# The second MLP product as seven block products

## The chip, the cores and the metric

The kernel runs on one core of one Trainium2 chip. The metric is the device time of one execution in microseconds (us). Lower is better.

## The reference

One layer of a hybrid decoder on a sequence of 512 tokens and a model width of 1,024, all in float32. Three token mixers (pooling, a gated convolution, dilated attention) feed a gated sum and the product with `w_o`. The change concerns what follows it:

```
x = x + merged @ w_o
h2 = rms_norm(x, norm_mlp)
x = x + jnp.square(jax.nn.relu(h2 @ w_ff1)) @ w_ff2      # w_ff1 1024 x 4096, w_ff2 4096 x 1024
```

## The kernel before, in words

Everything lies transposed, channels on the 128 partitions and the 512 tokens along the free dimension. Each float32 matmul is done as three in the `fp32r` type: a tile is split into a high part (a copy on ScalarE that rounds, `hi`) and a low part (a subtraction on VectorE, `lo`), and the product is high by high, high by low, low by high. `split` (L127) does this for a weight unit of 128 x 1024, into tiles `wh` and `wl` with three buffers each; `mm3` (L134) issues the three matmuls. Weight units come over SP's queue into `raw` tiles, three buffers.

The residual is `res`, eight tiles of 128 x 512. After the product with `w_o`, whose last four chunks (`wo_chunk`, 24 matmuls of 512 columns each) end one after the other, `x2_evac` (L682) adds a chunk to the residual on VectorE and writes a copy scaled by the norm's gain, `hs`, on ScalarE. `rs2.add` squares the residual on ScalarE and sums on VectorE.

The first MLP product (L781 to L840) is done by seven block products instead of eight, in eight groups of 512 hidden channels. The forms of the activations (P1, P2, Q3 to Q7, each a block or a sum of blocks of `hs`, split into high and low) are made once. For each group the forms of the weights are made as they go: B11, B12, B21 and B22 are the four 512 KB blocks of a group. One sum of two blocks is made on VectorE (`u`), three others by a DMA on POOL's queue that accumulates into the tile (`wx`, three buffers, or `wy`, two). `order()` gives the order of the products, `w_fill` makes forms `FORMS_AHEAD` (2) ahead of use, and `product` issues 24 matmuls of 256 columns: for eight 128 x 128 weight blocks the three of high and low. Evacuations follow Q6, Q7, P2 and Q4; they apply the relu, the norm and the square and leave the hidden activations `f` in SBUF. VectorE and ScalarE run in written order from the first `x2_evac` to Q4 of group 0; after that a planner orders them by its own costs.

The second MLP product (L820 to L862) is a plain one. For each of 32 tiles of `f` it loads a unit of `w_ff2`, splits both, and issues 8 x 3 matmuls of 512 columns into eight PSUM banks, one bank for each 128 output channels. Five banks of the first tile are begun between Q7 and Q4 of the last group (`EARLY`). The last three tiles are done bank by bank (`TAIL`), so that a bank can be added to the residual and stored while the next one is finished.

Of the kernel before, what the change touches and what calls it, by code (L numbers as in the profile page):

```python
# [18 lines left out]
P = 128  # L19
D = 1024  # L20
S = 512
# [45 lines left out]
def hybrid_layer(ctx: ExitStack, tc: tile.TileContext, xT, wst, pmix, vecs, consts, outT):  # L67
# [59 lines left out]
    def split(raw, pool):  # L127
        hi = pool.tile([P, 1024], F32R, tag="wh", name=nm("wh"))
        lo = pool.tile([P, 1024], F32R, tag="wl", name=nm("wl"))
# [401 lines left out]
    for m in range(KC):  # L531
        gt = []
        for n in range(3):
# [7 lines left out]
            pump()  # L541
        if m == 0:
# [4 lines left out]
            lp = right(front, "lp")  # L547
            for k in range(KC):
                t = rp.tile([P, S], F32, name=f"res{k}")
                nc.scalar.dma_start(t, xT[:, k, :])  # L550
                res.append(t)
# [38 lines left out]
    fpool = right(back, "fpool", reuse_waits="tile")  # L590
    sm = ExitStack()
# [20 lines left out]

    NG = NFF // 4

    def order():
# [7 lines left out]
        yield from [("Q6", NG - 1), ("Q4", NG - 2), ("Q7", NG - 1), ("Q4", NG - 1)]  # L623
# [7 lines left out]
    def w1_forms():  # L631
# [8 lines left out]
        for kind, g in order():  # L640
# [22 lines left out]
            elif kind == "Q4":  # L663
                yield xt[g]

    forms = w1_forms()
    ready = deque()

    def w_fill(n):
        while len(ready) < n:  # L670
# [3 lines left out]
            ready.append(split(t, wpool))  # L674

    def w_form():
        w_fill(FORMS_AHEAD + 1)
# [13 lines left out]
    def split_form(kind, t, ks, sign=1.0):  # L691
        if kind not in sx:
            sx[kind] = [spool.tile([P, 4, H], F32R, name=f"{kind}{part}") for part in "hl"]
# [37 lines left out]
    def late(kind, g):  # L731
# [7 lines left out]
        elif (kind, g) == ("Q5", 0):  # L739
            split_form("Q6", s2, HIGH)  # L740
            for m in range(5, KC):
# [37 lines left out]
    outs, fs, ws = [], [], []  # L779
    EARLY = 5  # L780
    for kind, g in order():  # L781
# [25 lines left out]
        elif kind == "Q6":  # L807
            q.R = bank()
            product(kind, q.R, True, True)
            q.v = tmp()  # L810
            nc.vector.tensor_tensor(q.v, q.R, q.x1, OP.subtract)
            nc.vector.tensor_tensor(q.f[:, 2:4, :H], halves(q.v), halves(q.T), OP.add)
        elif kind == "Q7":
# [6 lines left out]
            if g == NG - 1:  # L820
                n_loaded[0] = base + NFF
                end[0] = wst.shape[0]
                ws.append(unit())
                both = fpool.tile([P, 1024], F32R, tag="wx", bufs=3, name=nm("f0"))
# [131 lines left out]
```

## Time and profile before

| | |
|---|---|
| median of 3 runs | 819.49 us (819.14 to 821.77) |
| profiled execution | 818.48 us, of which the span from the first to the last instruction is 816.7 us |
| mean granted TensorE clock | 0.994 of full speed |
| TensorE / VectorE / ScalarE busy | 98% / 60% / 41% of the span |
| DMA | 93.66 MB, 115 GB/s over the span |

The span is what the views of the trace show, and the time of the execution is 1.8 us longer. PE is TensorE, PEld its weight loads, DVE VectorE, ACT ScalarE, POOL GpSimd and SP SyncE; a letter q behind an engine is its queue. An arrow `<-` stands between what an instruction writes and what it reads. In brackets behind an instruction stands how long its engine was idle before it, and which instruction released it.

### The profile page before, as it was taken

What the parts mean: (1) busy time and instruction counts of PE and PEld (TensorE: products, weight loads), DVE (VectorE), ACT (ScalarE), POOL (GpSimd) and SP (SyncE); (2) the same over time, 40 slices, a digit from 0 to 9 for tenths busy, and PEclk for the clock granted to TensorE, in tenths of its full rate; (3) what the DMA queues carried; (4) which work ended last, traced back from release to release, by engine and by line L of the source; (5) the groups of instructions that cost most, each with busy time, mean ns of one, the idle gap of its engine ahead of it and who ended that gap; (6) DMA issues with size and microseconds to landing.
All of it is one profiled execution on the core that took longest, in us unless ns stands there. A gap on an engine that the chain in (4) does not pass through costs nothing.

```text
span 816.7 us, 10396 instructions
## 1 busy us (share of the span) xinstructions
PE 801.2 (98%) x4225; PEld 679.9 (83%) x4225; DVE 488.3 (60%) x608; ACT 336.2 (41%) x432; POOL 71.9 (9%) x67
## 2 busy tenths in 40 slices
PE   8999998999999999999999989999999999999998
PEld 5787787887888888888888878999999888888886
DVE  7758686776895434543445588887777633233323
ACT  6375255742363222222222665555564433223320
POOL 4320012124200000000000011111110000000000
PEclk9999999999999999999999989999999999999999
DMA  7323221222244222333232266877775322332312
GB/s 253 129 79 104 77 78 52 91 84 72 78 147 164 77 85 101 101 103 102 78 103 78 104 170 139 234 183 187 187 181 115 130 86 95 104 98 83 103 52 103
DMA packets 28271, 93.66 MB, mean 115 GB/s; under 512 B 3264, under 2 KB 3520, under 8 KB 28224
## 3 DMA queue, kind: packets, MB, share of 16 engines
q1 hardware_dynamic: 23472, 78.19, 28.2%
q0 software_dynamic: 3456, 12.58, 9.3%
q10 hardware_dynamic: 1296, 2.23, 0.9%
q8 instruction: 33, 0.54, 0.3%
q14 instruction: 14, 0.11, 0.0%
HBM read 90.90 MB, written 2.10 MB: 114 GB/s over the span
## 4 chain that ended last, share of the span: by engine, by line
PE 89%; DVE 5%; ACT 3%; issue 2%; DMA 1%; SPq 0%; DVEq 0%; ACTq 0%
PE bank L137 23%; PE bank L138 23%; PE bank L139 23%; PE bank L761 5%; PE bank L760 5%; PE bank L762 5%; ACT wh L130 1%; DVE wl L131 1%; DMA mg<-xT 1%; DVE wl L233 1%; PE bank L393 1%; PE bank L357 1%; DVE xs L178 1%; ACT hs L684 0%; PE bank L392 0%
## 5 line engine op out<-in xcount | busy, mean ns | idle before, releaser
L130 ACT ACTIVATE wh<-raw 128x1024 fp32r<-128x1024 f32 x120 | 126.9, 1057 | 297.3 <-PE bank L138 156.1
L131 DVE TENSOR_TENSOR wl<-raw,wh 128x1024 fp32r<-128x1024 f32 x120 | 148.4, 1237 | 131.7 <-ACT wh L130 131.4
L137 PE MATMUL bank<-xs,wh 128*128 128x512 f32 x464 | 183.0, 395 | 1.1 <-ACT tmp L206 1.1
L139 PE MATMUL bank<-xs,wl 128*128 128x512 f32 x464 | 181.9, 392 | 1.3 <-DVE wl L233 1.2
L138 PE MATMUL bank<-xs,wh 128*128 128x512 f32 x464 | 182.2, 393 | 0.6 <-DVE xs L179 0.6
L137 PEld LDWEIGHTS bank<-xs,wh 128*128 128x128 f32 x464 | 87.1, 188 | 22.3 <-ACT tmp L206 1.6
L139 PEld LDWEIGHTS bank<-xs,wl 128*128 128x128 f32 x464 | 87.2, 188 | 21.4 <-DVE wl L233 2.5
L138 PEld LDWEIGHTS bank<-xs,wh 128*128 128x128 f32 x464 | 87.2, 188 | 19.9 <-DVE xs L179 1.3
L139 PE MATMUL bank<-tmp,wl 128*128 128x512 f32 x248 | 97.6, 394 | 0.0
L138 PE MATMUL bank<-tmp,wh 128*128 128x512 f32 x248 | 97.2, 392 | 0.0
L137 PE MATMUL bank<-tmp,wh 128*128 128x512 f32 x248 | 95.6, 389 | 0.0
L537 DVE TENSOR_TENSOR tmp<-bank,rstd 128x512 f32<-128x512 f32 x24 | 16.6, 692 | 66.8 <-PE bank L139 66.8
L138 PEld LDWEIGHTS bank<-tmp,wh 128*128 128x128 f32 x248 | 46.5, 188 | 11.0 <-DVE tmp L419 0.2
L137 PEld LDWEIGHTS bank<-tmp,wh 128*128 128x128 f32 x248 | 46.6, 188 | 10.3
L139 PEld LDWEIGHTS bank<-tmp,wl 128*128 128x128 f32 x248 | 46.5, 188 | 9.6 <-DVE wl L131 0.3
L130 ACT ACTIVATE wh<-wx 128x1024 fp32r<-128x1024 f32 x24 | 25.4, 1059 | 24.1 <-PE bank L761 22.4
L563 DVE TENSOR_TENSOR tmp<-tmp,bank 128x512 f32<-128x512 f32 x24 | 16.5, 688 | 26.5 <-PE bank L139 26.5
L138 PE MATMUL bank<-br,wh 128*128 128x512 f32 x80 | 31.4, 393 | 0.0
L137 PE MATMUL bank<-br,wh 128*128 128x512 f32 x80 | 31.3, 391 | 0.0
L648 POOL DMA_DIRECT2D wx<-wst x8 | 7.2, 900 | 273.2 <-DVE P2l L697 255.1
L139 PE MATMUL bank<-br,wl 128*128 128x512 f32 x80 | 31.1, 389 | 0.0
L131 DVE TENSOR_TENSOR wl<-wx,wh 128x1024 fp32r<-128x1024 f32 x24 | 29.3, 1222 | 2.2 <-ACT wh L130 1.7
(217 smaller groups left out, 1468.4 us busy)
## 6 DMA issues: line engine op xcount, KB each, us to landing
raw<-wst SPq DMA_DIRECT2D x128, 512.0 KB, 3.3
wx<-wst POOLq DMA_DIRECT2D x16, 512.0 KB, 5.7
wy<-wst SPq DMA_DIRECT2D x8, 512.0 KB, 5.1
wy<-wst POOLq DMA_DIRECT2D x8, 512.0 KB, 5.4
raw<-wst SPq DMA_DIRECT2D x8, 256.0 KB, 5.4
mg<-xT SPq DMA_DIRECT2D x8, 256.0 KB, 5.5
res<-xT ACTq DMA_DIRECT2D x8, 256.0 KB, 4.2
outT<-res SPq DMA_DIRECT2D x7, 256.0 KB, 2.0
```

The costliest lines, as they stand in the source:

```text
L130: nc.scalar.activation(hi, raw, AF.Copy)
L131: nc.vector.tensor_tensor(lo, raw, hi.bitcast(F32), OP.subtract)
L137: nc.tensor.matmul(out, wh[:, cols], xh, start=start, stop=False)
L138: nc.tensor.matmul(out, wh[:, cols], xl, start=False, stop=False)
L139: nc.tensor.matmul(out, wl[:, cols], xh, start=False, stop=stop)
L178: nc.vector.tensor_scalar(hi, raw, gain, None, op0=OP.mult)
L233: tc.keep_in_program_order(nc.vector.tensor_tensor(lo[:, half], raw_w[kk][:, half], hi[:, half].bitcast(F32), OP.subtract))
L537: nc.vector.tensor_tensor(t, b, rstd, OP.mult)
L563: nc.vector.tensor_tensor(t, t, b, OP.mult)
L760: nc.tensor.matmul(o, wh[:, w], xh[:, k], start=first, stop=False, skip_group_check=True)
L761: nc.tensor.matmul(o, wh[:, w], xl[:, k], start=False, stop=False, skip_group_check=True)
L762: nc.tensor.matmul(o, wl[:, w], xh[:, k], start=False, stop=last, skip_group_check=True)
```

## The change

The second MLP product is done by seven block products a group too. A group takes 512 hidden channels of `f` (four tiles of 128), its blocks are 256 channels by 256 tokens on the side of the activations, and 256 hidden by 512 output channels of `w_ff2` on the other. The activation forms are now made for each group: `a_sum` makes the differences on VectorE (q5, q6, q3, q7), `a_split` the high and low parts, five buffers each. The weight forms are made as in the first product, by the same generator, in a stream that goes on from one product into the other; `order()` is longer by 56 products, p1, q5, q6 and q4 of all groups first, then p2, q3 and q7. The four accumulators (A, T, R, X) fill two PSUM banks each and stay there over all groups. B22 of the second product is loaded into five buffers, two `wy` and three `wx`. Every fourth weight form of the new product goes into the tiles that the activation form Q7 had, so there are four buffers for them and three forms ahead.

From Q6 of the last group on, VectorE, ScalarE and TensorE run in written order. p1(0) lies between Q4 of group 6 and Q7 of group 7, and q5(0) between Q7 and Q4 of group 7. After the last group of p1 and q5, ScalarE copies A and T (`keep`). The evacuation of an accumulator adds it to quarters of the residual and stores them. q7 of the last two groups is done output chunk by output chunk.

At the first product's start, the scaled copies `hs` are made on VectorE by `tensor_scalar`, four chunks are evacuated before P1 is split and the fifth after it, sums of squares of the first four follow, and the table load of ScalarE goes from L710 to right behind the last sigmoid.

```diff
-    def split(raw, pool):
+    def split(raw, pool, tags=("wh", "wl"), **kw):
...
+        if m == KC - 1:
+            tc.keep_in_program_order(nc.scalar.preload_act_table_set("natural_log_exp_and_others"))
...
+            res_all = rp.tile([P, KC, S], F32, name="res")
...
-        yield from [("Q6", NG - 1), ("Q4", NG - 2), ("Q7", NG - 1), ("Q4", NG - 1)]
+        n = NG - 1
+        yield from [("Q6", n), ("Q4", n - 1), ("p1", 0), ("Q7", n), ("q5", 0), ("Q4", n)]
+        yield from [("p1", 1), ("q5", 1), ("q6", 0)]
+        for g in range(2, NG):
+            yield from [("p1", g), ("q5", g), ("q6", g - 1), ("q4", g - 2)]
+        yield from [("p2", 0), ("q6", n), ("q4", n - 1), ("q3", 0), ("p2", 1), ("q4", n), ("q3", 1), ("q7", 0)]
+        for g in range(2, NG):
+            yield from [("p2", g), ("q3", g), ("q7", g - 1)]
+        yield ("q7", n)
...
+            elif kind == "p1":
+                bt[g] = raw_unit()
+                nc.sync.dma_start(bt[g], w2_block(g, B11))
+                yield bt[g]
+            elif kind == "q5":
+                b12 = raw_unit()
+                nc.sync.dma_start(b12, w2_block(g, B12))
+                xt[g] = wx()
+                nc.vector.tensor_tensor(xt[g], bt[g], b12, OP.add)
+                yield xt[g]
+                nc.gpsimd.dma_start(xt[g], w2_block(g, B22), accum_op=OP.add)
+            elif kind == "q6":
+                yield xt[g]
+                nc.gpsimd.dma_start(xt[g], w2_block(g, B21), accum_op=OP.add)
+            elif kind == "q4":
+                yield xt[g]
+            elif kind == "p2":
+                z = raw_unit()
+                nc.sync.dma_start(z, w2_block(g, B21))
+                yield z
+            elif kind == "q3":
+                yt[g] = wy() if g in (0, 1, 5, 6) else wx()
+                nc.sync.dma_start(yt[g], w2_block(g, B22))
+                yield yt[g]
+                nc.gpsimd.dma_start(yt[g], w2_block(g, B12), accum_op=OP.add)
+            elif kind == "q7":
+                yield yt[g]
...
     def w_fill(n):
-        while len(ready) < n:
+        while len(ready) < n and (len(ready) < 3 or n_form[0] >= more):
...
-            ready.append(split(t, wpool))
+            k = n_form[0] - more
+            if k >= 0 and k % 4 == 0:
+                ready.append(split(t, late_forms, ("Q7h", "Q7l"), bufs=1))
+            else:
+                ready.append(split(t, wpool))
+            n_form[0] += 1
 
     def w_form():
-        w_fill(FORMS_AHEAD + 1)
+        w_fill(FORMS_AHEAD + (1 if opool is None else 2))
...
     def x2_evac(m):
         nc.vector.tensor_tensor(res[m], res[m], wo_banks[m], OP.add)
-        nc.scalar.activation(hs[m // 4][:, m % 4], res[m], AF.Copy, scale=vec[:, V_NF + m:V_NF + m + 1])
+        nc.vector.tensor_scalar(hs[m // 4][:, m % 4], res[m], vec[:, V_NF + m:V_NF + m + 1], None, op0=OP.mult)
...
-    tc.keep_in_program_order(nc.scalar.preload_act_table_set("natural_log_exp_and_others"))
...
-    for m in range(5):
+    for m in range(4):
         x2_evac(m)
     split_form("P1", a11, ALL)
+    x2_evac(4)
+    for m in range(4):
+        rs2.add(res[m], nc.vector)
     x2_evac(5)
-    for m in range(5):
-        rs2.add(res[m], nc.vector)
...
+    def a_split(kind, g):
+        hi, lo = (opool.tile([P, 2, H], F32R, tag=tag, bufs=5, name=nm(tag)) for tag in ("ah", "al"))
+        nc.scalar.activation(hi, sums[kind, g], AF.Copy)
+        nc.vector.tensor_tensor(lo, sums[kind, g], hi.bitcast(F32), OP.subtract)
+        return hi, lo
...
+    def a_fill(n):
+        while len(a_ready) < n and n_split[0] < len(second):
+            while n_sum[0] < min(n_split[0] + 2, len(second)):
+                a_sum(*second[n_sum[0]])
+                n_sum[0] += 1
+            a_ready.append(a_split(*second[n_split[0]]))
+            n_split[0] += 1
...
+        if w is None:
+            a_fill(FORMS_AHEAD + 2)
+            w, x = w_form(), a_ready.popleft()
+        (wh, wl), (xh, xl) = w, x
+        for c in chunks if chunks != range(4) else [None]:
+            for kk in range(2):
+                for cc in range(4) if c is None else [c]:
+                    o = banks[i][cc // 2][:, cc % 2 * H:(cc % 2 + 1) * H]
+                    wc = cols(4 * kk + cc)
+                    first, last = opens and kk == 0 and cc % 2 == 0, g == NG - 1 and kk == 1
+                    nc.tensor.matmul(o, wh[:, wc], xh[:, kk], start=first, stop=False, skip_group_check=True)
+                    nc.tensor.matmul(o, wh[:, wc], xl[:, kk], start=False, stop=False, skip_group_check=True)
+                    nc.tensor.matmul(o, wl[:, wc], xh[:, kk], start=False, stop=last, skip_group_check=True)
...
         elif kind == "Q6":
+            if g == NG - 1:
+                ordered = ExitStack()
+                ordered.enter_context(tc.manual_schedule(engines={
+                    mybir.EngineType.DVE, mybir.EngineType.Activation, mybir.EngineType.PE}))
             q.R = bank()
             product(kind, q.R, True, True)
+            if g == NG - 1:
+                sm.close()
+                opool = right(back, "opool", reuse_waits="tile")
+                a_fill(1)
...
         elif kind == "Q4":
             product(kind, q.R, False, True)
+            if g == NG - 2:
+                a_fill(FORMS_AHEAD)
...
+        elif kind == "q7" and g >= NG - 2:
+            a_fill(FORMS_AHEAD + 2)
+            held.append((w_form(), a_ready.popleft()))
+            if g == NG - 1:
+                for b in range(2):
+                    res_add(1, 1, b, snap["x1", b], OP.subtract)
+                    res_add(1, 0, b, snap["x1", b])
+                    res_add(1, 1, b, snap["x5", b])
+                    res_add(1, 0, b, pair(banks["X"][b]))
+                for b in range(2):
+                    for c in (2 * b, 2 * b + 1):
+                        for gg, (w, x) in zip((NG - 2, NG - 1), held):
+                            product2(kind, gg, [c], w, x)
+                    res_add(1, 1, b, pair(banks["R"][b]))
+                    store(1, 1, b, nc.sync)
+                    res_add(1, 0, b, pair(banks["R"][b]), OP.subtract)
+                    store(1, 0, b, nc.scalar)
...
+                    elif kind == "p2":
+                        res_add(0, 0, b, pair(banks["A"][b]))
+                        store(0, 0, b, nc.sync)
+                    elif kind == "q3":
+                        res_add(0, 1, b, pair(banks["T"][b]))
+                        store(0, 1, b, nc.sync)
...
-        if k < NFF - TAIL:
-            for m in range(EARLY if k == 0 else 0, KC):
-                mm3(outs[m], ws[k], cols(m), fs[k], k == 0, False)
-    for m in range(KC):
-        for k in range(NFF - TAIL, NFF):
-            mm3(outs[m], ws[k], cols(m), fs[k], False, k == NFF - 1)
-        parts = [slice(0, S)] if m < KC - 1 else [slice(0, S // 2), slice(S // 2, S)]
-        for t, eng in zip(parts, (nc.sync, nc.scalar)):
-            nc.vector.tensor_tensor(res[m][:, t], res[m][:, t], outs[m][:, t], OP.add)
-            eng.dma_start(outT[:, m, t], res[m][:, t])
```

Names in lower case (p1, q5 and so on) are the products of the second MLP product, those in upper case of the first; the number behind, as in q5(0), is the group. Where the text speaks of the first half of the new product it means p1, q5, q6 and q4 of all groups, and p2, q3 and q7 are the second half.

## Rows read from the trace of the kernel before

**Rows 1.** The page's first part: busy time, share of the span, instructions.
```profile
PE 801.2 (98%) x4225; PEld 679.9 (83%) x4225; DVE 488.3 (60%) x608; ACT 336.2 (41%) x432; POOL 71.9 (9%) x67
```

**Rows 2.** The page's fourth part: the chain that ended last, by engine.
```profile
PE 89%; DVE 5%; ACT 3%; issue 2%; DMA 1%; SPq 0%; DVEq 0%; ACTq 0%
```

**Rows 3.** Windows: length, busy PE, PEld, DVE, ACT, POOL, clock, DMA share, GB/s.
```profile
460.00:480.00 20.00, 17.40 (x92) 15.34 (x91) 15.45 (x20) 11.43 (x18) 0.51 (x1) 0.83 0.21 70
...
540.00:560.00 20.00, 20.00 (x172) 20.00 (x171) 15.30 (x17) 10.37 (x11) 2.59 (x3) 1.00 0.79 191
...
680.00:700.00 20.00, 20.00 (x89) 16.38 (x89) 7.20 (x8) 6.33 (x8) 0.00 (x0) 1.00 0.25 83
```

**Rows 4.** Timeline of TensorE: start, length, instruction, wait before it.
```profile
465.66 0.39 PE L137 MATMUL bank<-mg,wh 128*128 128x512 f32 x1
...
467.03 0.28 PE L760 MATMUL bank<-P1h,wh 128*128 128x256 f32 x1
...
469.74 0.28 PE L762 MATMUL bank<-P1h,wl 128*128 128x256 f32 x1
471.92 0.49 PE L760 MATMUL bank<-P1h,wh 128*128 128x256 f32 x1 [1.91 <-ACT wh L130]
...
488.80 1.12 PE L214 MATMUL bank<-tmp,ones 128*128 128x512 f32 x2
...
508.59 0.39 PE L760 MATMUL bank<-P1h,wh 128*128 128x256 f32 x1 [0.87 <-ACT wh L130]
```

**Rows 5.** Windows of 2 us at two waits of TensorE, columns as above.
```profile
474.00:476.00 2.00, 2.00 (x11) 2.00 (x11) 0.80 (x2) 1.24 (x3) 0.00 (x0) 0.50 0.64 262
508.00:510.00 2.00, 0.96 (x5) 0.74 (x6) 1.43 (x2) 1.49 (x2) 0.00 (x0) 1.00 0.00 0
```

**Rows 6.** Timeline of VectorE.
```profile
457.11 1.23 DVE L697 TENSOR_TENSOR P1l<-hs,P1h 128x1024 fp32r<-128x1024 f32 x1 [4.21 <-ACT P1h L695]
...
488.80 1.23 DVE L131 TENSOR_TENSOR wl<-wx,wh 128x1024 fp32r<-128x1024 f32 x1
...
509.71 1.22 DVE L638 TENSOR_TENSOR wx<-raw,raw 128x1024 f32<-128x1024 f32 x1
510.85 1.22 DVE L131 TENSOR_TENSOR wl<-wx,wh 128x1024 fp32r<-128x1024 f32 x1
511.99 0.68 DVE L834 TENSOR_TENSOR f<-tmp,bank 128x512 f32<-128x512 f32 x1
512.58 1.22 DVE L131 TENSOR_TENSOR wl<-wx,wh 128x1024 fp32r<-128x1024 f32 x1
...
520.99 0.69 DVE L771 SCALAR_TENSOR_TENSOR f<-bank,rstd 128x512 f32<-128x512 f32 x1 [0.31 <-PE bank L762]
...
608.62 0.69 DVE L834 TENSOR_TENSOR f<-tmp,bank 128x512 f32<-128x512 f32 x1 [0.16 <-PE bank L762]
609.34 0.69 DVE L771 SCALAR_TENSOR_TENSOR f<-f,rstd 128x512 f32<-128x512 f32 x1
...
631.23 0.69 DVE L834 TENSOR_TENSOR f<-tmp,bank 128x512 f32<-128x512 f32 x1 [0.28 <-PE bank L762]
...
812.95 0.75 DVE L861 TENSOR_TENSOR res<-res,bank 128x256 f32<-128x256 f32 x2 [1.38 <-PE bank L139]
```

**Rows 7.** Timeline of ScalarE.
```profile
439.49 1.06 ACT L130 ACTIVATE wh<-raw 128x1024 fp32r<-128x1024 f32 x1 [5.18 <-issue]
...
451.65 1.28 ACT L710 ACT_TABLE_LOAD   x1
452.95 3.18 ACT L684 ACTIVATE hs<-res,vec 128x512 f32<-128x512 f32 x5
...
511.05 1.06 ACT L130 ACTIVATE wh<-wx 128x1024 fp32r<-128x1024 f32 x1 [1.56 <-DVE wx L638]
```

**Rows 8.** The scaled split at the kernel's start, L178: shortest, median, longest, ns.
```profile
L178 DVE TENSOR_SCALAR xs<-mg,vec x8: 481/487/1532, 5.3 to 26.1; 128x512 fp32r<-128x512 f32 x8
```

**Rows 9.** DMA issues of accumulating loads: KB each, median us to landing.
```profile
wy<-wst POOLq DMA_DIRECT2D x8, 512.0 KB, 5.4
```

More of the change, by code (lines that the diff above doesn't have):

```diff
@@ L590, in hybrid_layer @@
     fpool = right(back, "fpool", reuse_waits="tile")
+    late_forms = right(back, "late_forms", reuse_waits="tile")
     sm = ExitStack()
@@ L740, in late @@
             split_form("Q6", s2, HIGH)
-            for m in range(5, KC):
+            for m in range(4, KC):
                 rs2.add(res[m], nc.vector)
@@ L778, in hybrid_layer, with block, pair, sub @@
     groups = [Group() for _ in range(NG)]
-    outs, fs, ws = [], [], []
-    EARLY = 5
+    def block(g, i):
+        c, t = i % 10 - 1, i // 10 - 1
+        return groups[g].f[:, 2 * c:2 * c + 2, t * H:(t + 1) * H]
+    def pair(ap):
+        return ap.rearrange("p (b t) -> p b t", b=2)
+    def sub(out, a, b):
+        nc.vector.tensor_tensor(out, a, b, OP.subtract)
+    sums = {}
+    def a_sum(kind, g):
+        if kind in ("q5", "q6"):
+            sums[kind, g] = opool.tile([P, 2, H], F32, tag=kind, bufs=2 if kind == "q5" else NG, name=nm(kind))
+        if kind == "q5":
+            sub(sums[kind, g], block(g, 21), block(g, 22))
+        elif kind == "q6":
+            sub(sums[kind, g], block(g, 11), sums["q5", g])
+        elif kind == "q3":
+            sums[kind, g] = sums["q6", g]
+            sub(sums[kind, g], block(g, 12), sums["q6", g])
+        elif kind == "q7":
+            sums[kind, g] = block(g, 21)
+            sub(sums[kind, g], block(g, 21), block(g, 11))
+        else:
+            sums[kind, g] = block(g, {"p1": 11, "p2": 12, "q4": 22}[kind])
@@ new lines, in a_split @@
+    def a_split(kind, g):
[3 more added lines that the diff above has]
+        return hi, lo
+    second = [x for x in order() if x[0].islower()]
+    a_ready = deque()
+    n_sum, n_split = [0], [0]
+    def a_fill(n):
[5 more added lines that the diff above has]
+            n_split[0] += 1
@@ L819, in hybrid_layer @@
             nc.scalar.activation(q.f[:, 2:4], q.f[:, 2:4], AF.Square)
[L820 to L824, printed above, removed]
-                fs.append((both[:, :S], both[:, S:]))
-                nc.scalar.activation(fs[0][0], groups[0].f[:, 0], AF.Copy)
-                nc.vector.tensor_tensor(fs[0][1], groups[0].f[:, 0], fs[0][0].bitcast(F32), OP.subtract)
-                for m in range(EARLY):
-                    outs.append(bank())
-                    mm3(outs[m], ws[0], cols(m), fs[0], True, False)
         elif kind == "Q4":
             product(kind, q.R, False, True)
+            if g == NG - 2:
+                a_fill(FORMS_AHEAD)
             c = q.f[:, 0:2, H:]
@@ L900, in _stream @@
             units.append(blocks[kh, :, :, ch].transpose(1, 2, 0, 3).reshape(P, 1024))
-    for k in range(NFF):
-        units.append(w_ff2[k * P:(k + 1) * P])
+    blocks = w_ff2.reshape(NFF // 4, 2, 2, P, 2, 4, P)
+    for g in range(NFF // 4):
+        for kh, ch in ((0, 0), (0, 1), (1, 1), (1, 0)):
+            units.append(blocks[g, kh, :, :, ch].transpose(1, 0, 2, 3).reshape(P, 1024))
     assert tuple(long) == LONG
```

63 lines of the change are left out of this document (44 added, 19 removed).

## The prediction

> **What bounds the kernel now.** I read the page first. TensorE is busy for 98% of the span, and the chain that ended last is 89% TensorE [rows 1, 2]. So time can come from fewer or shorter matmuls, or from places where TensorE waits or runs slowly. The windows say where those are: in the stretch of the first block products TensorE's loads fill every microsecond (PEld 20.00 of 20), in the second MLP product it streams 512-column matmuls and VectorE is mostly idle (7.20 of 20), and only around 460 to 480 us does TensorE stand still and the granted clock fall, to 0.83 on average [rows 3]. The order of TensorE's instructions gives two prices. Six 512-column matmuls start between 465.66 and 467.03, so one takes 0.2283 us; 24 of 256 columns make a product, whose first starts at 467.03 and whose last at 469.74, which is 2.71 / 23 = 0.1178 us each and 2.83 us a product [rows 4]. A 256-column matmul is therefore a little more than half a 512-column one.
>
> The same rows show the hole: 1.91 us of waiting at 471.92, and then matmuls at half rate. The granted clock is 0.50, the 1.2 GHz level, in 474 to 476, after that wait; near 508 waits of 0.87 and less leave it at 1.00 [rows 4, 5]. From 467.03 to the evacuation of the 15th product, at 520.99, pass 53.9 us [rows 4, 6]; 15 products at 2.83 and the 1.1 us that the sum-of-squares matmul takes make 43.5. The start of the block products thus loses 10.4 us.
>
> **Matmuls.** Removed: 32 x 8 x 3 = 768 matmuls of 512 columns, 175.3 us. Added: 8 groups x 7 products x 24 = 1,344 of 256, 158.3 us. That is 17.0 us less. Before, Q4 of group 6 ends at 631.1 [rows 6], the last matmul just before 812.95 [rows 6]: 181.8 us for Q7, Q4 and the second product, while 2 x 2.83 + 175.3 is 181.0. The 0.8 us of waits there go too: -17.8.
>
> **Vector and Scalar work for them.** VectorE starts long operations (1,024 elements) 1.14 us apart and short ones (512) 0.60 apart, though each lasts 1.22 and 0.69; a short one that reads the one before starts 0.72 after it [rows 6]. Where VectorE hands a tile to ScalarE and needs it back, it stands for about 1.3 us in the long case (a wx sum starts at 509.71, its ACT copy at 511.05 and lasts 1.06, less the 1.14 of the sum) [rows 6, 7]. A group of the first half of the new product (p1, q5, q6, q4) has four weight splits, one weight sum, four activation splits and two activation differences: 5 x 1.14 + 6 x 0.60 + 1.3 = 10.6 us, against 4 x 2.83 = 11.3 on TensorE. The second half (p2, q3, q7) has 3 x 1.14 + 5 x 0.60 = 6.4 against 8.5. So TensorE stays the bound there, by 0.7 us a group. ScalarE needs less in both. I take no loss, as the forms are made three products ahead.
>
> The rule against this: the Trainium skill's "VectorE: DVE Perf Modes", section "The DRAIN you can't avoid", says that a Vector instruction does not start before the pipe of the one ahead is empty. The rows disagree, since 509.71 to 510.85 is shorter than the 1.22 us that the instruction lasts [rows 6]. By that rule the group would come to 5 x 1.22 + 6 x 0.69 + 1.3 = 11.5, over TensorE's 11.3.
>
> **Transfers.** A group moves seven 512 KB blocks, three of them accumulating, as a group of the first product does at the same rate of products. An accumulating one lands 5.4 us after its issue [rows 9]. In both halves at least three other splits lie between the split that releases it and the one that needs it, 8.5 us. SP's loads wait for raw buffers, which the sum of q5 frees a group earlier. Cost: nothing, hidden by the products between; without that cover, 5.4 us for each one late.
>
> **The seam.** From Q6 of group 7 on, VectorE, ScalarE and TensorE run in written order, and the evacuations of the last four old products meet the first forms of the new one. I count from the first matmul of that Q6. Up to the weight form of q6(0) VectorE has ten long operations (seven weight splits, two sums, one relu) and 18 short (four differences, six splits, eight in evacuations): 10 x 1.14 + 18 x 0.60 + 0.6 for dependent pairs = 22.8, from 1.1 on. TensorE wants that form after eight products, 22.6. By work alone the loss is 1.3. But the written order also makes VectorE stand: twice for a square behind a relu and the activation split behind it (about 1.2 each, 1.75 after the long relu), and at each new weight sum (1.3). Queue by queue, q5(0)'s form is complete at 15.0 (TensorE wants it at 11.3), p1(1)'s at 22.5 (wanted at 17.0), q6(0)'s at 31.3, q5(2)'s at 37.2. Behind the waiting instructions are the evacuations of Q7 and Q4, and nothing needs those earlier. q6(1) and q4(0) are then in time. Loss at q5(2), 14 us into the new product: 8.7 us. Bounds 1.3 and 11.5, the latter if the clock falls at the last wait too. After the first wait, some 2.5 us and so longer than the one of 1.91 [rows 4], I expect it to fall; those slow products end before the next form is ready, and cost nothing.
>
> **The tail.** The last split waits for its accumulating block: q3(7)'s split 2.4 us after q3(6) starts, issue and landing 5.6 more, then copy and subtraction; ready at 10.4, wanted at 12.0. No wait for TensorE, but the evacuation of p2(7) is queued behind it. So VectorE then owes two, two and eight short additions, finishes them 0.9 us after the last matmul, and four more follow: it ends 3.4 us after TensorE, where before two quarter-size additions end 0.8 after [rows 6]. +2.6; bounds 0.5 (all but the last two hidden) and 4.
>
> **The start.** The eight scaled copies leave ScalarE, where five take 3.18 us behind a 1.28 us table load; the load goes to where ScalarE sat idle 5.18 us [rows 7], so it costs nothing. On VectorE such an operation has a median of 487 ns [rows 8], about 0.40 from start to start by the 0.09 that short ones overlap; 8 x 0.40 = 3.2 us, hidden in waits like the 4.21 us before 457.11 [rows 6]. Without that cover it would be 3.2. Following the new order: VectorE reaches the sixth addition at about 456.5, P1(0)'s form is complete at 458.8, P1(1)'s at 466.8 (TensorE wants it at 469.9, so hole and slow clock go), Q5(0)'s at 472.5, Q3(0)'s at 479.6 (wanted at 478.4), and Q6(0)'s subtraction starts at 483.3, where the trace has 488.80 [rows 6]. The order behind it is the same, so -5.5; bounds 0 and -10.4, the whole loss above. Late next is Q3(0)'s form, by about 1.2.
>
> **Sum.** -17.8 + 8.7 + 2.6 - 5.5 = -12.0. The profiled execution took 818.48 (span 816.7); the median of the runs is 819.49, 1.0 more. So 806.5 profiled, 807.5 in the median.
>
> **Rivals.**
> - The seam costs only its excess of work, 1.3: 800.1. For it: TensorE has forms ahead. Against it: written order leaves VectorE nothing to do while ScalarE holds a square. Chance 0.17.
> - The start gains nothing, since VectorE becomes there what ScalarE was: 813.0. For it: the new order gives VectorE 3.2 us more there. Against: it stood 4.21 us at one place alone [rows 6]. Chance 0.15.
> - Vector operations cost their whole durations: in the seam 10 x 0.08 + 18 x 0.09 = 2.4 and in the first half 0.2 x 8 = 1.6 more, 811.5. Against it are the starts in [rows 6]. Chance 0.07. The section of the Trainium skill named above would give this case.
> - The other side: VectorE pays the hand-off to ScalarE at every form of the first half, because the 1.06 us copy of a form is never made ahead. Then 4 x 1.14 + 4.74 + 4 x 1.15 = 13.9 us a group instead of 11.3, 8 x 2.6 = 20.8 more: 828.3, slower. It decides from three of four forms on (12.0 / 8 = 1.5 a group above 11.3). Against it: in 540 to 560 VectorE is busy 15.30 and TensorE never waits [rows 3]. Chance 0.08.
> - It doesn't do what it says: new matmuls take 175.3 / 1,344 = 0.130 us or more, as PEld is already full [rows 3]: 824.5. Against it, the form is the one measured at 0.1178. Chance 0.03.
>
> **Numbers.** The forecast has 0.50 and its own range is 803 to 812, from the seam's and the start's partial bounds. The range 799.5 to 815 takes in the first three rivals except their outer edges and leaves out the two slow ones and these edges, 0.2 in all. A measurement here tells 0.3%, 2.5 us, from no change: faster 0.85, same 0.05, slower 0.10 (the last two rivals give 0.11, the start's edge most of the 0.05).
>
> **What would show it.** In the changed profile: no half clock near 475 and Q6(0) about 5.5 us earlier; products 2.83 us apart in the new stage; waits of TensorE, 7 to 10 us in all, between q5(0) and q5(2), each behind a wl or wh; a VectorE that ends 3 to 4 us after the last matmul. Wrong it would be if TensorE waited in every group, if matmul starts lay further apart than 0.1178, or if the seam showed no wait.

## The result and the profile after

The changed kernel takes 811.21 us in the median of four runs (808.65 to 814.22), the kernel before 819.32 beside it (818.37 to 821.77). The ratio is 0.990, its 95% interval 0.9876 to 0.9924: 8.1 us faster, where 12.0 were predicted. The profiled execution took 810.79, of which 809.0 are the span, 7.7 less than before.

I cut each span at three places that all kernels here have: the first matmul of P1(0), the first one behind Q4(6) (p1(0) in the kernel after, Q7(7) in the kernel before), and the end of the last matmul.

| | P1(0) starts | P1(0) to p1(0) | p1(0) to the end of the last matmul | from there to the end |
|---|---|---|---|---|
| before | 467.03 | 164.0 | 181.9 | 3.8 |
| after | 468.18 | 164.0 | 169.6 | 7.3 |
| difference | +1.2 | 0.0 | -12.3 | +3.5 |
| predicted | 0 | -5.5 | -9.1 (-17.8 + 8.7) | +2.6 |

The 1.2 us ahead of P1(0) can't be laid to the change: among this kernel and its twelve variants below, which differ little up to there, P1(0) starts between 465.14 and 470.10. So I compare stretches, not spans.

The page's first part, of the kernel after:

```profile
PE 784.3 (97%) x4801; PEld 694.3 (86%) x4801; DVE 569.0 (70%) x715; ACT 369.3 (46%) x476; POOL 92.1 (11%) x91
```

Windows of the kernel after (columns as in [rows 3]):

```profile
472.00:476.00 4.00, 2.26 (x10) 2.26 (x11) 3.46 (x5) 0.44 (x1) 0.00 (x0) 0.71 0.57 183
540.00:560.00 20.00, 20.00 (x172) 20.00 (x171) 15.36 (x18) 10.57 (x13) 2.59 (x3) 1.00 0.79 198
640.00:644.00 4.00, 2.86 (x13) 2.66 (x14) 3.61 (x4) 1.27 (x2) 0.86 (x1) 0.62 0.85 274
644.00:648.00 4.00, 4.00 (x21) 4.00 (x21) 2.07 (x4) 2.52 (x3) 0.00 (x0) 0.53 0.66 119
700.00:720.00 20.00, 20.00 (x176) 20.00 (x175) 17.59 (x21) 11.94 (x17) 3.46 (x4) 1.00 0.84 200
```

TensorE is busy for 97% of the span, after 98% in [rows 1]. Its two holes are at 471 to 474, near that of [rows 4], and ahead of 640.38, in the seam; the granted clock falls to 0.71 behind the first and to 0.62 and 0.53 behind the second. In the new product it starts 176 matmuls in 20 us, in the first product 172. VectorE, 7.20 of 20 us busy in the second product before [rows 3], now has 17.59.

Timeline of TensorE, kernel after:

```profile
468.18 0.28 PE L810 MATMUL bank<-P1h,wh 128*128 128x256 f32 x1
...
473.74 0.58 PE L812 MATMUL bank<-P1h,wl 128*128 128x256 f32 x1 [2.34 <-DVE wl L130]
...
640.38 0.38 PE L900 MATMUL bank<-ah,wh 128*128 128x256 f32 x1 [2.42 <-ACT wh L129]
...
662.54 0.38 PE L900 MATMUL bank<-ah,wh 128*128 128x256 f32 x1 [0.65 <-ACT wh L129]
...
663.80 0.38 PE L902 MATMUL bank<-ah,wl 128*128 128x256 f32 x1 [0.76 <-DVE wl L130]
...
688.82 0.28 PE L900 MATMUL bank<-ah,wh 128*128 128x256 f32 x1
...
690.97 0.28 PE L901 MATMUL bank<-al,wh 128*128 128x256 f32 x1
...
691.20 0.28 PE L900 MATMUL bank<-ah,wh 128*128 128x256 f32 x1
...
691.56 0.28 PE L900 MATMUL bank<-ah,wh 128*128 128x256 f32 x1
```

The wait at P1(1) of [rows 4], 1.91 us, is there again with 2.34, now for VectorE. The seam's waits are at q5(0) (2.42, and 0.76 at 641.64), p1(2) (0.20 at 659.02) and q5(2) (0.65 and 0.76), and none follows. Of q6(3), 19 steps lie between 688.82 and 690.97: 0.1132 us a matmul. With q4(2), at 691.20, a step is 0.12.

Timeline of VectorE, kernel after:

```profile
446.18 0.69 DVE L732 TENSOR_TENSOR res<-res,bank 128x512 f32<-128x512 f32 x1 [0.81 <-PE bank L138]
448.69 1.23 DVE L130 TENSOR_TENSOR wl<-raw,wh 128x1024 fp32r<-128x1024 f32 x1 [1.83 <-ACT wh L129]
452.81 1.23 DVE L130 TENSOR_TENSOR wl<-raw,wh 128x1024 fp32r<-128x1024 f32 x1 [2.89 <-ACT wh L129]
453.95 0.48 DVE L733 TENSOR_SCALAR hs<-res,vec 128x512 f32<-128x512 f32 x1
454.35 0.68 DVE L732 TENSOR_TENSOR res<-res,bank 128x512 f32<-128x512 f32 x1
...
463.37 0.68 DVE L732 TENSOR_TENSOR res<-res,bank 128x512 f32<-128x512 f32 x1
...
631.34 1.22 DVE L130 TENSOR_TENSOR wl<-wy,wh 128x1024 fp32r<-128x1024 f32 x1
632.47 0.68 DVE L868 TENSOR_TENSOR al<-q,ah 128x512 fp32r<-128x512 f32 x1
...
637.94 1.22 DVE L686 TENSOR_TENSOR wx<-raw,raw 128x1024 f32<-128x1024 f32 x1
640.36 2.36 DVE L130 TENSOR_TENSOR wl<-wx,wh 128x1024 fp32r<-128x1024 f32 x2 [1.20 <-ACT wh L129]
...
646.95 0.69 DVE L868 TENSOR_TENSOR al<-q,ah 128x512 fp32r<-128x512 f32 x1 [1.64 <-ACT ah L867]
...
662.51 1.23 DVE L130 TENSOR_TENSOR wl<-wx,wh 128x1024 fp32r<-128x1024 f32 x1 [1.21 <-ACT wh L129]
...
794.30 1.23 DVE L130 TENSOR_TENSOR wl<-wx,wh 128x1024 fp32r<-128x1024 f32 x1 [3.41 <-ACT wh L129]
...
802.05 3.07 DVE L909 TENSOR_TENSOR res<-res,bank 128x512 f32<-128x512 f32 x5
```

At the start, the first scaled copy (L733) comes 7.8 us behind the first addition: two subtractions for the weights of `wo_chunk` 6 and 7 stand between them, each after an idle wait. Only then do the second addition and the rest follow. In the seam VectorE stands at the hand-offs to ScalarE that the prediction listed. At the end sixteen additions run from 795.45 on without a gap.

### The profile page after: what moved, and what is told of

Its sections match the earlier page's. It is cut to its first block, busy times and chain, and to the rows that moved or that the text cites. A ratio compares the mean times of both kernels' runs of the same rounds, so it can differ in the third digit from the quotient of the medians.

```text
span 809.0 us, 11818 instructions
## 1 busy us (share of the span) xinstructions
PE 784.3 (97%) x4801; PEld 694.3 (86%) x4801; DVE 569.0 (70%) x715; ACT 369.3 (46%) x476; POOL 92.1 (11%) x91
## 4 chain that ended last, share of the span: by engine, by line
PE 52%; issue 30%; DVE 7%; POOL 4%; DMA 3%; ACT 2%; SPq 0%; POOLq 0%; DVEq 0%; ACTq 0%
PE bank L136 16%; PE bank L137 16%; PE bank L138 16%; DMA wx<-wst 3%; DVE wl L130 1%; ACT wh L129 1%; DVE res L909 1%; POOL wx L673 1%; POOL wx L691 1%; POOL wx L688 1%; DMA mg<-xT 1%; DVE wl L232 1%; PE bank L356 1%; PE bank L392 1%; POOL wy L670 1%
## 5 line engine op out<-in xcount | busy, mean ns | idle before, releaser
L138 PE MATMUL bank<-xs,wl 128*128 128x512 f32 x464 | 181.9, 393 | 1.3 <-DVE wl L232 1.2
L900 PE MATMUL bank<-ah,wh 128*128 128x256 f32 x448 | 125.7, 281 | 3.1 <-ACT wh L129 3.1
L902 PE MATMUL bank<-ah,wl 128*128 128x256 f32 x448 | 126.0, 281 | 1.7 <-DVE wl L130 1.7
L901 PE MATMUL bank<-al,wh 128*128 128x256 f32 x448 | 125.4, 280 | 0.0
L900 PEld LDWEIGHTS bank<-ah,wh 128*128 128x128 f32 x448 | 85.5, 191 | 3.5 <-ACT wh L129 3.5
L129 ACT ACTIVATE wh<-wx 128x1024 fp32r<-128x1024 f32 x56 | 59.0, 1056 | 64.7 <-DVE wx L686 25.4
L902 PEld LDWEIGHTS bank<-ah,wl 128*128 128x128 f32 x448 | 85.6, 191 | 2.3 <-DVE wl L130 2.3
L901 PEld LDWEIGHTS bank<-al,wh 128*128 128x128 f32 x448 | 85.5, 191 | 0.0
L130 DVE TENSOR_TENSOR wl<-wx,wh 128x1024 fp32r<-128x1024 f32 x56 | 68.3, 1222 | 21.1 <-ACT wh L129 20.4
L130 DVE TENSOR_TENSOR wl<-wy,wh 128x1024 fp32r<-128x1024 f32 x24 | 29.2, 1221 | 6.5 <-ACT wh L129 6.5
L137 PE MATMUL bank<-br,wh 128*128 128x512 f32 x80 | 31.4, 393 | 0.0
```

The costliest lines, as they stand in the source:

```text
L137: nc.tensor.matmul(out, wh[:, cols], xl, start=False, stop=False)
L138: nc.tensor.matmul(out, wl[:, cols], xh, start=False, stop=stop)
L900: nc.tensor.matmul(o, wh[:, wc], xh[:, kk], start=first, stop=False, skip_group_check=True)
L901: nc.tensor.matmul(o, wh[:, wc], xl[:, kk], start=False, stop=False, skip_group_check=True)
L902: nc.tensor.matmul(o, wl[:, wc], xh[:, kk], start=False, stop=last, skip_group_check=True)
```

## The experiments

Each changes the kernel after in one place unless it says more. The stretches of all, one profile each; the last column is the median where a number of runs stands, and otherwise the one run that there is:

| | P1(0) starts | to p1(0) | to the start of the last matmul | to the end | execution |
|---|---|---|---|---|---|
| after | 468.18 | 163.96 | 169.35 | 7.51 | 810.79 |
| e1 additions first | 469.20 | 161.82 | 169.36 | 7.32 | 807.95, 4 runs |
| e2 copies on ScalarE | 467.72 | 164.53 | 169.36 | 7.29 | 809.96, 4 runs |
| e3 loop orders | 467.80 | 163.98 | 169.55 | 7.47 | 810.47, 4 runs |
| e4 fourth slot | 466.05 | 163.97 | 169.40 | 7.38 | 808.59 |
| e5 sum ahead | 465.14 | 164.01 | 164.33 | 7.32 | 803.32 |
| e6 squares deferred | 467.59 | 163.98 | 169.57 | 7.46 | 810.47 |
| e7 tail additions | 466.84 | 163.99 | 169.54 | 5.13 | 807.31 |
| e8 sums on GpSimd | 468.92 | 161.37 | 169.34 | 7.77 | 810.78 |
| e9 three pairs | 469.92 | 163.97 | 175.23 | 7.68 | 818.60 |
| e10 short waits | 466.88 | 166.70 | 169.34 | 7.58 | 812.38 |
| x1 | 470.10 | 161.34 | 164.32 | 5.14 | 802.65, 4 runs |
| x2 | 467.95 | 161.40 | 161.97 | 5.18 | 799.20, 5 runs |

The last matmul counts from its start here, 0.28 us ahead of its end in the table above, and "to the end" goes by spans given to 0.1 us. A kernel with an edit in one stretch has the others within 0.3 us, so differences of more than that are read from one profile each.

**e1, additions first.**

```diff
-    for m in range(4):
-        x2_evac(m)
+    for m in range(4):
+        x2_add(m)
+    for m in range(4):
+        x2_scale(m)
```

`x2_add` and `x2_scale` are the two lines of `x2_evac`.

> Edit: the four additions of the residual (m = 0 to 3) are written ahead of the four scaled copies, instead of each before its copy. In the changed kernel VectorE stands idle 1.83 and 2.89 us at 446.9 and 449.9, and three additions (0.72 each, 2.15 us) run only after the last weight subtraction of the output projection. Theory A (the start is bound by VectorE's order and work): the additions fall into the idle time, P1's low form and all behind it come 2.15 us earlier against the start of P1(0), TensorE's wait of 2.34 us at 473.74 all but goes, and the stretch from P1(0) to the end of Q4(6), 163.96 us, falls by 2 to 4; the kernel is 2 to 4 us faster than the changed one (807 to 809). Rival B (something else, a transfer or ScalarE, sets Q6(0)'s form): the forms may come earlier but the stretch moves by 0.5 us or less.

Timeline of VectorE of e1:

```profile
447.20 2.48 DVE L732 TENSOR_TENSOR res<-res,bank 128x512 f32<-128x512 f32 x4 [0.82 <-PE bank L138]
449.72 1.23 DVE L130 TENSOR_TENSOR wl<-raw,wh 128x1024 fp32r<-128x1024 f32 x1
453.84 1.23 DVE L130 TENSOR_TENSOR wl<-raw,wh 128x1024 fp32r<-128x1024 f32 x1 [2.89 <-ACT wh L129]
454.98 1.67 DVE L735 TENSOR_SCALAR hs<-res,vec 128x512 f32<-128x512 f32 x4
...
459.63 0.49 DVE L735 TENSOR_SCALAR hs<-res,vec 128x512 f32<-128x512 f32 x1
...
463.35 1.22 DVE L130 TENSOR_TENSOR wl<-raw,wh 128x1024 fp32r<-128x1024 f32 x1
```

A window of e1:

```profile
472.00:476.00 4.00, 3.19 (x26) 2.79 (x24) 3.23 (x6) 1.57 (x3) 0.00 (x0) 1.00 0.72 262
```

The additions fill the first wait, the four copies run together behind the second subtraction, and the stretch is 2.14 us shorter, with the clock at 1.00 where it was 0.71. Theory A, at its lower end. The sixth addition starts at 462.23, against P1(0) 2.2 us earlier than in the kernel after, which is what the stretch gains. The kernel's ratio to before is 0.9876 (0.9857 to 0.9896); this interval overlaps that of the kernel after, so it is the stretch that shows the gain.

**e2, the copies back on ScalarE.**

```diff
-        nc.vector.tensor_scalar(hs[m // 4][:, m % 4], res[m], vec[:, V_NF + m:V_NF + m + 1], None, op0=OP.mult)
+        nc.scalar.activation(hs[m // 4][:, m % 4], res[m], AF.Copy, scale=vec[:, V_NF + m:V_NF + m + 1])
```

> Edit: the scaled copies of the residual go back to ScalarE; all else as in the changed kernel (that part of the change undone alone). By the prediction's start term the stretch from P1(0) to the end of Q4(6) gets 5.5 us longer (169.5). Theory A (moving the copies gained nothing because VectorE's additions between the copies lie behind the two weight subtractions): 163.96 within 0.7, since the additions then stand ahead of the subtractions again. Rival: VectorE is freed of 8 x 0.40 us of copies and nothing waits for ScalarE, 1 to 3 us shorter.

164.53: undoing that part costs 0.6 us, within theory A's bound. The copies' move was worth 0.6, not 5.5. The ratio is 0.9911 (0.9882 to 0.9940).

**e8, three sums of squares on GpSimd, with e1's edit.**

```diff
-        rs2.add(res[m], nc.vector)
+        rs2.add(res[m], nc.gpsimd)
```

> Edit: as the run with the additions first, and besides that three of VectorE's additions of squares (2.28 us at 460) are done on GpSimd, which is idle there. That run left waits of TensorE of 0.69, 1.44, 0.55, 0.47 and 0.83 us between 476 and 489. Theory A (the start is bound by what VectorE has to do in its order): all forms up to Q6(0)'s come 2.28 us earlier and the stretch from P1(0) to Q4(6)'s subtraction (162.76 there, 164.89 in the changed kernel) falls by 1.8 to 2.5 more. Rival B (behind e1 ScalarE or the transfers set those waits): 0.5 or less.

161.37, 0.45 less than e1 (162.29 against 162.76 by the subtraction of Q4(6)). That is the number of rival B, but the trace doesn't bear out its reason. GpSimd and VectorE of e8:

```profile
458.58 4.18 POOL L209 TENSOR_TENSOR tmp<-tmp,tmp 128x512 f32<-128x512 f32 x3 [232.31 <-ACT tmp L205]
459.35 0.82 DVE L735 TENSOR_SCALAR hs<-res,vec 128x512 f32<-128x512 f32 x1
...
461.53 2.32 DVE L130 TENSOR_TENSOR wl<-raw,wh 128x1024 fp32r<-128x1024 f32 x1
```

While GpSimd adds, VectorE's two copies take 0.82 us each where e1 has 0.49, and the subtraction behind them, at 461.53, takes 2.32 where e1 has 1.22 (463.35). So 1.8 of the 2.28 us that left VectorE come back as longer instructions, and the rest is what the stretch gains. x1 and x2 have the same long instructions. TensorE's waits of 0.61 and 1.44 at 475.34 and 477.28 stay. Both are for copies of ScalarE, which works without a gap from 473.70 on, where it had waited 5.04 us for a difference of VectorE. So theory A, that VectorE's order and work set the start, isn't refuted here; taking work off VectorE without putting it on GpSimd wasn't tried.

**e5, the weight sum one form earlier.**

```diff
             elif kind == "p1":
                 nc.sync.dma_start(bt[g], w2_block(g, B11))
+                b12 = raw_unit()
+                nc.sync.dma_start(b12, w2_block(g, B12))
+                xt[g] = wx()
+                nc.vector.tensor_tensor(xt[g], bt[g], b12, OP.add)
                 yield bt[g]
```

The same lines leave the branch of q5.

> Edit: in the second half the weight sum of q5 (B11 + B12) is written ahead of the split of p1's block of the same group, no longer right before its own split. In the changed kernel VectorE stands 1.20 (640.36), 1.21 (651.46) and 1.21 us (662.51) between such a sum and the subtraction that needs ScalarE's copy of it; p1's subtraction (1.14) would now lie there. Theory H (part of the seam's loss of 8.8 us is hand-offs between VectorE and ScalarE): nine products from Q4(6)'s end take 34.2 - 2.4 to 3.6 us, and the kernel is 2 to 3.6 us faster than the changed one. Rival W (VectorE's work and the transfers set the seam): the sum now waits for both blocks' loads, and the seam changes by under 0.7 us or gets longer.

Windows of e5:

```profile
640.00:644.00 4.00, 2.41 (x19) 2.00 (x17) 2.46 (x3) 2.98 (x4) 0.00 (x0) 1.00 0.24 47
644.00:648.00 4.00, 3.44 (x29) 3.44 (x30) 3.90 (x5) 1.49 (x2) 1.63 (x2) 1.00 0.78 254
```

Timeline of VectorE of e5:

```profile
642.15 1.22 DVE L684 TENSOR_TENSOR wx<-raw,raw 128x1024 f32<-128x1024 f32 x1
643.28 1.22 DVE L130 TENSOR_TENSOR wl<-raw,wh 128x1024 fp32r<-128x1024 f32 x1
644.58 2.36 DVE L130 TENSOR_TENSOR wl<-wx,wh 128x1024 fp32r<-128x1024 f32 x2
...
653.99 1.22 DVE L130 TENSOR_TENSOR wl<-wx,wh 128x1024 fp32r<-128x1024 f32 x1
```

The hand-off is covered by another split, and the stretch falls by 5.0 us, more than theory H's 3.6. TensorE waits 1.03, 0.60 and 1.55 us instead of 2.42, 0.76, 0.20, 0.65 and 0.76, and the clock stays at 1.00 in the windows that had 0.62 and 0.53. The prediction had the slow clock of the seam cost nothing, and the traces agree. The subtraction for q5(2), the last form that was late, starts 30.4 us behind the first matmul of p1(0) in the kernel after (662.51) and 24.8 in e5 (653.99). Between p1(0) and there, no idle time of VectorE or ScalarE ends with TensorE in either kernel, so the form came 5.5 us earlier by the order of these two engines and not by TensorE's pace. In the kernel after TensorE still had to wait for it.

**e6, relu and squares of the last evacuations deferred.**

```diff
+            if kind == "q4" and g < 3:
+                finish(*rest.popleft())
```

`finish` does relu and square of Q4(6), Q7(7) and Q4(7) in turn; they leave the evacuations of these products.

> Edit: the relu and square of Q4(6), Q7(7) and Q4(7) (VectorE 0.61, 1.14 and 0.61 us, ScalarE three of 1.06) are done after q4(0), q4(1) and q4(2) instead of in the seam; the subtractions that free the banks stay. Theory H (the squares stand in front of ScalarE's copies and VectorE waits for those, 1.04 at 636.12, 1.64 at 646.95, 1.04 at 656.79): the seam's 34.2 us fall by 4 to 6. Theory W (only VectorE's own work counts): by 2.0 to 2.8. Rival: the deferred work makes forms of the groups behind late; the seam falls but the products after it get as much longer, and the time stays within 1.

169.57: the rival. From p1(0) to the end of Q4(7) the run takes 13.05 instead of 17.65, and from there to the last matmul 156.52 instead of 151.70. TensorE waits again in groups 3 to 6. Timeline of VectorE of e6 around 680:

```profile
679.06 1.22 DVE L130 TENSOR_TENSOR wl<-wx,wh 128x1024 fp32r<-128x1024 f32 x1 [1.21 <-ACT wh L129]
```

Timeline of TensorE of e6:

```profile
680.34 0.38 PE L902 MATMUL bank<-ah,wl 128*128 128x256 f32 x1 [0.76 <-DVE wl L130]
```

So the prediction's 10.6 us of VectorE's work against 11.3 of TensorE's in a group is right in that there is next to no room: work that leaves the seam must find it, and the hand-off at 679.06 is still there.

**e7, eight additions earlier.**

```diff
+            if kind == "p2" and g in (2, 4):
+                b = g // 2 - 1
+                res_add(1, 1, b, snap["x1", b], OP.subtract)
+                res_add(1, 0, b, snap["x1", b])
...
```

The other four follow after p2(3) and p2(5), and all eight leave their place ahead of the last matmuls.

> Edit: eight of VectorE's last sixteen additions, those that need nothing of the last two products (the saved copies of products 1 and 5 and the bank of product 4), are done after p2(2) to p2(5) instead of after the last product's form. In the changed kernel the sixteen run back to back from 795.45 to 805.8 and TensorE ends at 801.6. Theory T (the tail of 7.4 us behind TensorE's end is VectorE's backlog): TensorE's end to the span's end falls by 2.4 to 2.9. Rival S (the last stores' issue and landing set the end): by 0.5 or less.

VectorE of e7 at the end:

```profile
794.30 2.48 DVE L909 TENSOR_TENSOR res<-res,bank 128x512 f32<-128x512 f32 x4
797.96 1.28 DVE L909 TENSOR_TENSOR res<-res,bank 128x512 f32<-128x512 f32 x2 [1.19 <-PE bank L902]
800.68 1.28 DVE L909 TENSOR_TENSOR res<-res,bank 128x512 f32<-128x512 f32 x2 [1.44 <-PE bank L902]
```

VectorE waits for TensorE now, where before TensorE's results waited for VectorE. The stretch is 2.4 us shorter: theory T. From VectorE's end (801.96) to that of the span (805.5) remain 3.5.

**e3, e4, e9, e10: the step from one matmul to the next.** The new product ran faster than 0.1178 us a matmul, which the prediction hadn't foreseen. e3 swaps the two loops in both products:

```diff
-        for b in range(2):
-            for k in range(4):
+        for k in range(4):
+            for b in range(2):
...
-            for kk in range(2):
-                for cc in range(4) if c is None else [c]:
+            for cc in range(4) if c is None else [c]:
+                for kk in range(2):
```

> Edit: in a product of the first MLP half the loop over k goes outside the loop over the two output halves (as in the second half's product the moving tile stays for several matmuls); in the second half's product the loop over the four outputs goes outside the loop over the two k (as in the first half's, one output region is accumulated in a row). All else as in the changed kernel. Measured there: 0.1178 us from one matmul to the next in the first half, 0.1133 in three of four products of the second half. Theory L (the pitch follows the loop order): first half 0.1133, 56 products x 24 x 0.0045 = 6.0 us less, second half 0.1178 throughout, about 4 us more. Rival S (it follows the buffers or something else that the loops don't touch): 0.1178 and 0.1133 as before, time 811 within 2.

First product 0.1178 (172, 172 and 173 in 20 us), new one 0.1133 and each fourth product 0.1200, as without the swap: rival S, the loops have no part.

e4 puts the fourth pair at another place in the sequence, and in turn two pairs of tiles:

```diff
-            if k >= 0 and k % 4 == 0:
-                ready.append(split(t, late_forms, ("Q7h", "Q7l"), bufs=1))
+            if k >= 0 and k % 4 == 2:
+                ready.append(split(t, late_forms, ("Q4h", "Q4l") if k // 4 % 2 else ("Q7h", "Q7l"), bufs=1))
```

> Edit: in the second half the products whose weight form lies in a fourth pair of tiles outside the weight pool are those with number 2, 6, 10, ... from q6(0) on instead of 0, 4, 8, ..., and they take turns between two pairs of tiles (that of Q7's forms and that of Q4's). In the changed kernel each fourth product, with its form in Q7's pair, takes 0.1179 to 0.120 us a matmul and all others 0.1133. Theory B (the place of the weight form sets it): products 2, 6, 10, ... are the slow ones. Rival P (the position in the sequence, or which product it is): 0, 4, 8, ... stay slow. If only every eighth is slow, the one pair of tiles is the cause and the other not.

The slow products (0.1200) are now 6, 10, 14 and so on, with either pair of tiles. That agrees with theory B. e9 drops the fourth pair:

```diff
-        while len(ready) < n and (len(ready) < 3 or n_form[0] >= more):
+        while len(ready) < min(n, 3):
...
-            if k >= 0 and k % 4 == 0:
-                ready.append(split(t, late_forms, ("Q7h", "Q7l"), bufs=1))
-            else:
-                ready.append(split(t, wpool))
+            ready.append(split(t, wpool))
```

> Edit: the fourth pair of tiles for weight forms is left out; all forms of the second half lie in the weight pool's three pairs, made at most three products ahead. Theory B (forms outside the weight pool make a product slow): no product behind the seam at 0.1196 us a matmul, all at 0.1133, 12 x 24 x 0.0063 = 1.8 us less behind Q4(7). Rival D (the fourth pair is what hides VectorE's form making): VectorE has 0.7 us of slack a group and a form may now start only when a product ends, so waits of 0.5 to 1.5 us come back in each of the six groups, 3 to 9 us more.

Both theories fall. A window of e9:

```profile
700.00:720.00 20.00, 20.00 (x172) 20.00 (x171) 16.66 (x20) 10.34 (x13) 2.59 (x3) 1.00 0.74 166
```

No wait comes back in the groups (one of 0.76 at 804.59), but every product up to there runs at 0.1178, with all forms in the weight pool: 172 matmuls in 20 us, not 176. From q6(1) to q7(7) that makes 3.2 us and the late matmul 1.3, and the seam is 1.4 longer. So without the fourth pair not only the 0.1200 is gone but the 0.1133 too; with four pairs in turn the mean is 0.115, with three 0.1178. The last idea was that a short wait in a product sets the faster step:

```diff
-        nc.vector.tensor_tensor(lo, raw, hi.bitcast(F32), OP.subtract)
+        for _ in range(1 + extra):
+            nc.vector.tensor_tensor(lo, raw, hi.bitcast(F32), OP.subtract)
```

`extra` is 2 for P2(3) and P2(5), else 0.

> Edit: in the first half, for the form of P2(3) and of P2(5) VectorE does its subtraction three times instead of once, so that TensorE has to stand for about 1 us in each of these products, at the first matmul that uses the low form. Seen so far: matmuls of 256 columns follow each other at 0.1178 us through the first half, but at 0.1132 in Q3(0), right behind a wait of 0.45 us for a low form (486.33), and at 0.1133 in the last product of e9, right behind the only such wait there (804.59), while all the products ahead of it ran at 0.1178. Theory S (such a short wait sets the faster pitch and it lasts): products behind the first forced wait run at 0.1133, up to 30 x 24 x 0.0045 = 3.2 us given back until Q4(6). Rival N (only the product with the wait, or none): 0.1178 in the products behind, and the stretch P1(0) to p1(0), 163.96, gets longer by the two waits, about 2 us.

TensorE waited 1.39 us at 539.57 and 0.82 at 580.24, and all products behind kept 0.1178: rival N. The stretch grew by 2.7.

The traces show one thing more. In all thirteen the step, once it is there, stays from product to product, in e9 over 49 of them. It changes only at a product whose form lies in the fourth pair, or in which a matmul comes late (more than 0.126 us behind the one ahead). Behind a late matmul it comes out either way: behind the waits of q5(2), q6(1) runs at 0.1133 in the kernel after and at 0.1178 in e7, whose edit lies far behind it. And four pairs alone don't make it: in x2, below, seven products behind the seam run at 0.1178 without a wait, among them q6(4), 23 steps long here:

```profile
688.33 0.28 PE L908 MATMUL bank<-ah,wh 128*128 128x256 f32 x1
...
691.03 0.28 PE L910 MATMUL bank<-ah,wl 128*128 128x256 f32 x1
```

What sets the step there stays open; four pairs in the first product weren't tried.

**x1 and x2.** x1 joins e8 (with e1), e5 and e7; x2 adds e6.

> Edit: the four changes that each shortened their stretch, together: additions of the residual first and three sums of squares on GpSimd (stretch to p1(0) 161.37 against 163.96), the weight sum of q5 ahead of p1's split (p1(0) to the last matmul 164.33 against 169.35), eight of the last additions earlier (tail 5.13 against 7.51). If the three stretches are independent, 2.6 + 5.0 + 2.4 = 10.0 us less than the changed kernel, 801.2. Rival: the stretches overlap in what they save (a form that is earlier at one place waits at the next), 804 to 806.

x1's stretches are those of e8, e5 and e7, each within 0.03 us: they are independent. The median, 802.65, is 1.5 above the sum, with P1(0) at 470.10 in its profile; the ratio to before is 0.9802 (0.9787 to 0.9817).

> Edit: x1 and the deferred relu and squares of e6. In e6 the seam fell by 4.6 us and the groups behind it gave 4.8 back, with VectorE at 0.7 us of slack a group. Theory V (VectorE's slack in the groups behind the seam decided that): with the q5 hand-off of 1.2 us gone VectorE has some 1.9 us of slack a group, the 2.4 us deferred fit in, and the 3.2 us of waits left in e5's seam (1.03, 0.60, 1.55) mostly go: 2 to 3 us less than x1, about 798.5. Rival G (deferred work costs as much behind as it saves in front, whatever the slack): within 0.7 of x1.

Windows of x2:

```profile
636.00:640.00 4.00, 4.00 (x36) 4.00 (x36) 3.89 (x6) 1.33 (x3) 0.00 (x0) 1.00 0.83 154
640.00:644.00 4.00, 4.00 (x36) 4.00 (x36) 4.00 (x6) 2.95 (x4) 1.73 (x2) 1.00 0.86 257
```

The only wait of TensorE behind p1(0), timeline of x2:

```profile
694.78 0.38 PE L910 MATMUL bank<-ah,wl 128*128 128x256 f32 x1 [0.35 <-DVE wl L130]
```

Theory V: the seam has no wait left, and the groups behind take the deferred work now that VectorE needn't stand at the weight sum. 799.20, ratio to before 0.9765 (0.9749 to 0.9781), which lies clear of x1's: 12.0 us less than the changed kernel by the medians, 11 by the ratios.

## Why the prediction came out as it did

**Matmuls, -17.8.** Right in kind, mis-sized: the step is 0.115 in the mean of the new product, not 0.1178. Nine products of the seam aside, 49 take 135.2 us instead of 49 x 24 x 0.1178 = 138.5, so the term is -21.1. e9 shows that nearly all of these 3.3 us go with the fourth pair. This gain was not foreseen and covers part of what the start lost, which is luck. That each fourth product lies further apart than 0.1178 was named as a sign of being wrong; the other three outweigh it. The rival of 0.130 us a matmul is out.

**The seam, +8.7.** The nine products from p1(0) to q5(2) take 34.3 us, 8.8 more than 9 x 24 x 0.1178 = 25.4, with waits at q5(0) and q5(2), as counted queue by queue. The rival that it costs only its excess of work is out. The waits make 4.8 us, not the 7 to 10 of the prediction's signs, because TensorE spent part of the time in matmuls 0.21 us apart while the clock was at 0.62 and 0.53. That the fall of the clock costs nothing agrees with the traces (see e5); no run tested it by itself.

**The start, -5.5: the step that failed.** It is "VectorE reaches the sixth addition at about 456.5". It starts at 463.37, 462.2 less the later start-up. In VectorE's order the two weight subtractions of `wo_chunk` 6 and 7 stand ahead of the first copy, and each waits for ScalarE. In the kernel before the same two stand there, but behind four of the additions:

```profile
445.03 2.48 DVE L683 TENSOR_TENSOR res<-res,bank 128x512 f32<-128x512 f32 x4 [0.82 <-PE bank L139]
447.55 1.23 DVE L131 TENSOR_TENSOR wl<-raw,wh 128x1024 fp32r<-128x1024 f32 x1
...
451.67 1.23 DVE L131 TENSOR_TENSOR wl<-raw,wh 128x1024 fp32r<-128x1024 f32 x1 [0.23 <-ACT wh L130]
```

The forms behind are late by that much, so neither the hole near 475 nor the slow clock went, and the second rival's outcome holds (the start gains nothing). Its reason, VectorE at its limit, isn't the whole: VectorE was idle 4.7 us at these two places. Putting the additions back in front makes the sixth 2.2 us earlier and gives 2.1 (e1); 5.7 us earlier was the prediction's for its 5.5. The copies ahead of the second subtraction weren't tried.

**The tail, +2.6.** Right mechanism (e7), 0.9 too small: VectorE ends 3.4 us behind TensorE, as predicted, but from there to the span's end pass 3.9, before 3.0.

**Other terms.** No group waits behind the seam, so VectorE's overlap and the transfers stood as argued, and the rival on the other side is out. The rival by the Trainium skill's "VectorE: DVE Perf Modes", "The DRAIN you can't avoid", gave 811.5, near what was measured, but not by that way: a subtraction at 631.34 lasts 1.22 and the next one starts 1.13 later. That section of the Trainium skill adds that a next operation which is not held starts earlier, which the prediction left out; the trace agrees. The sum with the measured terms is -21.1 + 8.8 + 3.5 + 0.0 = -8.8, and +1.2 of start-up makes, but for rounding, the -7.7 of the spans.

## What to carry to other kernels

When work moves to another engine, write down that engine's whole queue at that place, with what is ahead of the moved instructions, before counting a gain: moving was worth 0.6 us here, and the order of four additions 2.1. Before moving work to GpSimd, look what VectorE does beside it: of 2.28 us taken off VectorE, 1.8 came back in its neighbours (e8). At a seam in written order, put another split between a sum and the split that needs the other engine's copy of it; that gave 5.0 us. Work deferred out of a tight place helps only if the place that receives it has slack: the same deferral gave nothing, and 2.4 us once the hand-off was gone.

## What the runs showed of the hardware

The step between 256-column matmuls that never wait is not one number: 0.1178 us with three pairs of weight tiles in turn, and mostly 0.1133 in three products of four and 0.1200 in the fourth with four pairs, the same for either loop order. It stays through a product and from one product to the next until a form from the fourth pair or a late matmul comes. Single products took the faster step with three pairs too (Q3(0) of the kernel after, 0.1132 behind a wait at 486.33), and two waits made for it (e10) didn't bring it about.

While GpSimd added two SBUF tiles (458.58 to 462.76 in e8), VectorE's scaled copies took 0.82 us instead of 0.49 and a subtraction 2.32 instead of 1.22; an addition that reads a PSUM bank kept its 0.68.
